# Layer 0's first modulation chunks by pairs of feature tiles, and a 512-column projection between them

## The chip, the core and the metric

The kernel runs on one core of a Trainium2 chip. A core has a matrix engine (PE, whose weight loads are listed as PEld), a vector engine (VectorE, DVE), a scalar engine (ScalarE, ACT), a general engine (GpSimd, POOL) and SyncE (SP), which issues the DMA transfers. The metric is device time in microseconds (us), median over runs.

## The reference

Two transformer layers over 512 latent tokens and 256 context tokens, 1024 features. In each layer an input projection feeds an attention part and a gated MLP part; then come an output projection, and a squared-ReLU MLP. Both normalisations are modulated: shift, scale and gate are computed from a conditioning vector by one large matrix `w_mod`.

```python
m_lat = silu(c) @ w_mod[l] + b_mod[l]          # 6 x 1024: sh1, sc1, ga1, sh2, sc2, ga2
m_ctx = silu(c_ctx) @ w_mod[l] + b_mod[l]
h_lat = rmsnorm(x_lat, norm1_g[l]) * (1 + sc1) + sh1
h_ctx = rmsnorm(x_ctx, norm1_g[l]) * (1 + csc1) + csh1
z = h @ w_in[l]                                 # 512 q | 128 k | 128 v | 512 u | 512 g
q, k = rope(rmsnorm(q)), rope(rmsnorm(k))       # rope on latents alone
attn = softmax(q k^T) v                         # latents see all keys, context sees context
gm = gelu(u) * (w_s @ layernorm(gelu(g)) + b_s) # mixing inside chunks of 128 tokens
x = x + ga1 * (concat(attn, gm) @ w_out[l])
x = x + ga2 * (relu(modulate(rmsnorm(x))) ** 2 @ ...)   # w_ff1, w_ff2
```

## The kernel before

The residual `X` lies feature by token: eight tiles of 128 features x 768 tokens (512 latents, 256 context), two in each of four buffers. Every product is made at near float32 precision from three matmuls: each operand is split into a high and a low part (`hi`, `lo`), and hi x hi, hi x lo and lo x hi are summed in PSUM. A weight block of 128 x 1024 is loaded as `raw`; `split` casts it to `hi` on ScalarE and subtracts on VectorE to get `lo`. `block_order` writes down in which order blocks are loaded; `pump` issues the loads on SP while fewer than `RING` = 4 blocks are live, `take` hands them out, `release` gives them back. The first blocks go into buffers that are free at the start (`EARLY`, buffers A, B, C). In the start phase splits are held back (`held`) and made by `convert`.

PSUM has three pools of two buffers: `pa` (two banks each), `pb` and `pt` (one bank each).

`mod_chunk(l, j)` multiplies 512 columns of layer 0's `w_mod`, eight matmuls in float32 (two PE instructions each), with the conditioning vectors as the 32 columns of the weights. So several run side by side in PE's column groups: two for the first four chunks (`NS` = 2), four for the others. VectorE transposes the sums, eight tiny matmuls with a selection matrix (`fin`) bring the result into feature order, and `mod_store` adds the bias and makes `Amod` = (1 + scale) * gain. Chunks 0 and 1 are the shift of features 0 to 511 and 512 to 1023, chunks 2 and 3 the scale.

`Norm` makes one normalisation: squares on ScalarE (`step`), added up over the eight feature tiles on VectorE or POOL (`acc`); `sums` adds over partitions by one-column matmuls against `ones` and takes the reciprocal root; `bcast` spreads it over partitions; `apply` makes the modulated `h` tile by tile (VectorE, then a cast on ScalarE to the high part, then VectorE for the low part).

`start`, whose PE and VectorE order is that of the program text, runs: squares and `acc` of the latents, chunk 0, `sums`, chunk 2, first weight block, `apply` of tiles 0 to 3, chunk 1, then chunk 3 in quarters with the projection of keys and values (256 columns, `TokProj.wide`) for tiles 0 to 3 between them, then `apply` and projection of tiles 4 and on. After it the scheduler orders the engines by priority (the order of the text) and readiness.

`layer` then runs PLAN[0]: latent parts of u tiles 0 and 1 (`w0`, `w1`), context part of tile 0 (`x0`), keys and values of context (`kv`), the g projections A0 to B2 by pairs of token tiles with u tiles between, and after them the queries in two groups of 256 columns, three `bank` calls each. A bank is one PSUM buffer: `pt` if `self.early`, else `pb`; `self.early` is true if `kv0` is None when the projection is made, which holds before for the first one alone. Each bank goes to a sink: `qk` (normalisation of heads and rotation), `sink_g` (gelu, layer norm, later `mixing` into a `pt` buffer). Keys and queries are stacked (`stack`) and transposed (`turn`, two `pt` buffers) some 10 us later by the kernel's own clock `fl`.

Of the kernel before, what the change touches and what calls it, by code (L numbers as in the profile page):

```python
# [117 lines left out]
EARLY = [f"A{i}" for i in range(7, 3, -1)] + [f"B{i}" for i in range(7)] + ["C0", "C1"] + [f"A{i}" for i in range(7, 3, -1)]  # L118
PLAN = (("w0", "w1", "x0", "kv", "A0", "u2", "A1", "A2", "x1", "B0", "B1", "B2"),
# [3 lines left out]
def block_order():  # L123
    o = []
    mod = lambda j: [("mod", 0, j, kb) for kb in range(0, 4, 1 if j < 4 else 2)]
    tok = lambda l, g: [("tok", l, g, kb) for kb in range(2)]
    for l in range(DEPTH):
        if l == 0:
            o += mod(0) + mod(2) + tok(0, 0)[:1] + mod(1) + mod(3) + [("ctx",)] * (not PAR["XO"]) + tok(0, 0)[1:] + [("ctx",)] * PAR["XO"]
# [7 lines left out]
        o += tok(l, 1) + tok(l, 2)  # L137
# [24 lines left out]
    return o  # L162
# [3 lines left out]
def trunk(ctx: ExitStack, tc: tile.TileContext, xT, pk1, pk2, rope, wsT, w_mod, w_tok, w_u, w_out, w_ff1, w_ff2, outT):  # L166
# [53 lines left out]
    RING = 4  # L220
# [110 lines left out]

    def mod_chunk(l, j, lag=1200.0):
# [3 lines left out]
        ns = PAR["NS"] if j < 4 else 4  # L336
        rows = ns * 32
        for kb in range(0, 4, ns // 2):
            ws_ = take("mod", l, j, kb)[:ns // 2]
# [18 lines left out]
        if lag:  # L358
            fl.defer(lag, fin)
        else:  # L360
            fin()
# [48 lines left out]
    def mod_store(l, j, src, nc_=2):  # L410
        b0 = PK1["bmod"][0] + l * 48 + j * 4
# [21 lines left out]
    class Norm:  # L433
# [5 lines left out]
        def step(self, k):  # L439
# [6 lines left out]
            sq = (tw if self is cx and PAR['SQ'] else tsm)([128, n])  # L446
# [4 lines left out]
        def sums(self, *others):  # L451
# [55 lines left out]
    class TokProj:  # L507
        def __init__(self, l, grp, h, npair, sink):
            self.h, self.npair, self.sink, self.left = h, npair, sink, npair
            self.key = ("tok", l, grp)  # L510
            self.wb = {}
            self.early = PAR["BK"] == 1 and kv0 is None

        def passes(self, k):
            if k // 4 not in self.wb:
                self.wb[k // 4] = take(*self.key, k // 4)
# [36 lines left out]

    DENSE = {0: ((0, 384), (384, 384)), 1: ((0, 512),)}
# [17 lines left out]
    def consts(l):  # L572
        k2 = const.tile([128, 640], F32, tag="k2", name=nm("k2"))
        nc.scalar.dma_start(k2, pk2[l])
# [17 lines left out]
        vec.tensor_scalar_mul(P2("bs"), P2("bs"), 0.5)  # L592
# [5 lines left out]
    def layer(l, h, nxt, K, kv=None, kv0=0):  # L598
# [11 lines left out]
        def qk(ps4, tp, nh, which):  # L610

            sq = tsm([128, 2, nh, 64])
            act.activation(sq, ps4, AF.Square)
# [3 lines left out]
            if tp < 2:  # L617
# [6 lines left out]
                (pool_e if l in PAR['R1'] else vec).tensor_tensor(out=t1, in0=t1, in1=t2, op=ALU.add)  # L624
# [4 lines left out]
            r = rsqrt(ss, 2 * nh, l)  # L629
            (pool_e if l in PAR['R2'] else vec).tensor_tensor(out=t1, in0=t1, in1=r.rearrange("p (a b) -> p a b", b=nh).unsqueeze(3).broadcast_to([128, 2, nh, 64]), op=ALU.mult)  # L630
# [76 lines left out]
        def u_part(m, part):  # L707
# [4 lines left out]
            ps = (pt if PAR["BK"] == 2 and m and not part else pb)()[:, 0:n]  # L712
# [376 lines left out]
    def start():  # L1089
        nonlocal held  # L1090
        for k in range(KT):
            lat.step(k)
        run(mod_chunk(0, 0, PAR["S0"]))
        lat.sums()
        run(mod_chunk(0, 2, PAR["S2"]))
        convert()
        lat.bcast()
        fl.tick(PAR["S2"])
        lat.apply(h0, range(4))
        kv0.passes(0)  # L1100
        run(mod_chunk(0, 1, PAR["S1"]))
        for k in range(KT if PAR['CL'] == 0 else 0):
            cx.step(k)
        g = mod_chunk(0, 3, 1.0)
        for k in range(4):
            next(g)
            if k == 3:
                convert()
            kv0.wide([k])
            fl.tick()  # L1110
        fl.tick(1.0)
        lat.apply(h0, range(4, KT), lambda k: convert() if k == 6 else None)
        for k in range(KT if PAR['CL'] == 1 else 0):
            cx.step(k)
        if PAR["CS"] == 0:
            cx.sums()
        kv0.wide(range(4, PAR["KB"]))
        if PAR["CS"] == 1:
            cx.sums()

    if PAR["KF"]:
        pump()
# [3 lines left out]
    kv0 = TokProj(0, 0, h0, 3, None)  # L1126
    ET = mybir.EngineType
    MSS = {1: {ET.PE}, 2: {ET.PE, ET.Activation}, 3: {ET.PE, ET.DVE}, 4: {ET.PE, ET.DVE, ET.Activation}}
    if PAR["MS"]:
        with tc.manual_schedule(engines=MSS[PAR["MS"]]):  # L1130
            start()
    else:
        start()
# [6 lines left out]
    layer(0, h0, h1, K0, kv0, PAR["KB"])  # L1140
# [6 lines left out]
def _layout(x, c, ctx, c_ctx, w_mod, b_mod, norm1_g, w_in, q_norm_g, k_norm_g, gmlp_norm_g, w_spatial, b_spatial,  # L1147
# [20 lines left out]
    o["w_mod"] = C(A(w_mod).reshape(L, 4, 2, 128, 12, 512).transpose(0, 4, 1, 3, 2, 5).reshape(L, 12, 4, 128, 1024))  # L1168
# [4 lines left out]
    o["w_tok"] = C(wt.reshape(L, 2, 4, 128, 5, 256).transpose(0, 4, 1, 3, 2, 5).reshape(L, 5, 2, 128, 1024))  # L1173
# [25 lines left out]
```

## Time and profile before

| | |
|---|---|
| median of 3 runs | 1500.83 us (1500.49 to 1501.65) |
| profiled execution, first to last instruction | 1500.4 us |
| its instructions | 22327 |
| PE busy | 1460.4 us (97%) |
| VectorE busy | 893.1 us (60%) |
| ScalarE busy | 640.1 us (43%) |
| POOL busy | 340.4 us (23%) |
| moved by DMA | 148.80 MB, mean 99 GB/s |

The profiled execution is one run of the program; its own time is the span, and the runs' times are 0.1 to 1.3 us longer. A timeline row is: start, length, engine, line, operation, output <- inputs, shape, number of instructions merged; in brackets the idle time of the engine before it and what ended that. A row of the waits is: who waited for whom, total us, times, longest. `PEclk` is the clock granted to PE as a share of full speed. Tile names leave out buffer numbers: `A<-in_w_mod` is a load of modulation weights into a buffer A.

### The profile page before, as it was taken

How to read it: one execution, taken by the hardware profiler on the slowest of the kernel's cores; microseconds unless marked ns; L12 is line 12 of the kernel's file. 1: busy time of each engine (PE TensorE's matmuls, PEld its weight loads, DVE VectorE, ACT ScalarE, POOL GpSimd, SP SyncE). 2: the span in 40 equal slices, each digit the busy share in tenths (PEclk: the TensorE clock that was granted, in tenths of full speed). 3: DMA queues.
4: the chain of work that ended last, by engine and by line, in shares of the span. 5: the costliest groups of instructions: out<-in, count | busy, mean ns of one | idle time of the engine just before them, and what ended most of it. 6: DMA issues, size and time to landing. Idle time of an engine off the chain costs nothing.

```text
span 1500.4 us, 22327 instructions
## 1 busy us (share of the span) xinstructions
PE 1460.4 (97%) x8770; PEld 1286.8 (86%) x8770; DVE 893.1 (60%) x1667; ACT 640.1 (43%) x1078; POOL 340.4 (23%) x324
## 2 busy tenths in 40 slices
PE   6899999999999999999999999999999999999998
PEld 2899887798889999898989988997889888888887
DVE  5878767787755554544444436866877544444443
ACT  3443455674545443424334224536774333322221
POOL 0112331222064452313232213156222000000000
PEclk9999999999999999999999999999999999999999
DMA  9221454201233333433333311321001323333331
GB/s 365 65 77 38 175 182 146 90 15 57 74 118 116 112 115 116 131 109 123 117 115 124 99 43 57 99 71 57 29 1 57 114 97 98 99 99 99 99 96 73
DMA packets 49945, 148.80 MB, mean 99 GB/s; under 512 B 5424, under 2 KB 6832, under 8 KB 49840
## 3 DMA queue, kind: packets, MB, share of 16 engines
q1 hardware_dynamic: 49264, 146.46, 29.5%
q8 instruction: 69, 1.13, 0.3%
q10 hardware_dynamic: 576, 0.92, 0.2%
q14 instruction: 36, 0.29, 0.1%
HBM read 145.26 MB, written 2.10 MB: 98 GB/s over the span
## 4 chain that ended last, share of the span: by engine, by line
PE 88%; DVE 4%; DMA 2%; POOL 2%; ACT 2%; issue 1%; SPq 0%; POOLq 0%; ACTq 0%; DVEq 0%
PE pa L208 52%; PE pb L208 27%; PE pt L877 3%; PE pt L208 2%; PE pb L343 1%; PE pt L648 1%; DMA raw<-in_w_tok 1%; DMA B<-in_w_mod 1%; POOL acc L449 1%; DMA A<-in_w_mod 1%; DVE A L483 1%; DVE s L487 1%; DVE X L817 1%; POOL m L289 0%; DVE B L997 0%
## 5 line engine op out<-in xcount | busy, mean ns | idle before, releaser
L208 PE MATMUL pa<-A,hi 128*128 128x384 f32 (+2 forms) x1696 | 449.2, 347 | 2.1 <-DVE s L702 0.8
L212 ACT CAST hi<-raw 128x1024 fp32r<-128x1024 f32 x171 | 179.5, 1050 | 464.5 <-PE pa L208 378.7
L213 DVE TENSOR_TENSOR lo<-raw,hi 128x1024 fp32r<-128x1024 f32 x155 | 195.8, 1263 | 230.9 <-ACT hi L212 227.5
L208 PEld LDWEIGHTS pa<-A,hi 128*128 128x128 f32 x1696 | 304.4, 188 | 26.4 <-ACT w L990 2.0
L208 PE MATMUL pa<-A,lo 128*128 128x384 f32 (+2 forms) x848 | 293.5, 346 | 1.1 <-DVE lo L213 1.1
L208 PE MATMUL pa<-B,hi 128*128 128x512 f32 (+1 forms) x900 | 239.7, 355 | 2.7 <-DVE X L817 2.7
L387 POOL TENSOR_TENSOR C<-C,s 128x512 f32<-128x512 f32 x112 | 162.9, 1469 | 316.3 <-ACT s L386 275.6
L208 PEld LDWEIGHTS pa<-B,hi 128*128 128x128 f32 x900 | 158.7, 188 | 30.7 <-DVE X L817 4.9
L208 PEld LDWEIGHTS pa<-A,lo 128*128 128x128 f32 x848 | 159.4, 188 | 12.1 <-DVE lo L213 1.5
L817 DVE SCALAR_TENSOR_TENSOR X<-pa,modT,X 128x512 f32<-128x512 f32 x126 | 82.9, 660 | 141.8 <-PE pa L208 141.8
L208 PE MATMUL pb<-B,hi 128*128 128x512 f32 (+1 forms) x600 | 157.8, 351 | 3.8 <-DVE X L817 3.8
L208 PE MATMUL pa<-B,lo 128*128 128x512 f32 (+1 forms) x450 | 157.7, 354 | 0.0
L208 PE MATMUL pb<-hi,A 128*128 128x256 f32 x672 | 126.4, 285 | 0.8 <-DVE s L702 0.8
L817 DVE SCALAR_TENSOR_TENSOR X<-pb,modT,X 128x512 f32<-128x512 f32 (+3 forms) x116 | 71.0, 619 | 85.4 <-PE pb L208 85.0
L208 PEld LDWEIGHTS pb<-B,hi 128*128 128x128 f32 x600 | 105.0, 191 | 18.4 <-DVE X L817 5.3
L208 PEld LDWEIGHTS pb<-hi,A 128*128 128x128 f32 x672 | 106.2, 191 | 1.0 <-PE pb L208 1.0
L208 PE MATMUL pb<-B,lo 128*128 128x512 f32 (+1 forms) x300 | 104.9, 350 | 0.0
L386 ACT ACTIVATE s<-k,silu 128x512 f32<-128x512 f32 x112 | 76.8, 716 | 45.3 <-DMA k<-in_w_mod 36.2
L208 PE MATMUL pb<-lo,A 128*128 128x256 f32 x336 | 95.1, 283 | 0.0
L208 PEld LDWEIGHTS pa<-B,lo 128*128 128x128 f32 x450 | 84.0, 188 | 11.3
L208 PE MATMUL pb<-A,hi 128*128 128x512 f32 (+2 forms) x288 | 81.5, 363 | 2.1 <-POOL A L808 2.1
L880 DVE TENSOR_TENSOR A<-pt,A 128x384 fp32r<-128x384 f32 (+1 forms) x144 | 73.0, 536 | 10.5 <-ACT A L879 8.9
(176 smaller groups left out, 2209.5 us busy)
## 6 DMA issues: line engine op xcount, KB each, us to landing
raw<-in_w_ff SPq DMA_DIRECT2D x128, 512.0 KB, 3.5
k<-in_w_mod SPq DMA_DIRECT2D x96, 256.0 KB, 3.1
raw<-in_w_tok SPq DMA_DIRECT2D x19, 512.0 KB, 3.4
raw<-in_w_out SPq DMA_DIRECT2D x16, 512.0 KB, 3.5
lo<-in_w_mod SPq DMA_DIRECT2D x16, 512.0 KB, 4.6
hi<-in_w_mod SPq DMA_DIRECT2D x16, 512.0 KB, 3.9
A<-in_w_mod SPq DMA_DIRECT2D x8, 512.0 KB, 9.7
raw<-in_w_u SPq DMA_DIRECT2D x8, 512.0 KB, 3.4
```

Of the source, the lines that this page charges most:

```text
L208: pe.matmul(out, a, b, start=start, stop=stop)
L212: act.copy(hi, src)
L213: (eng or vec).tensor_tensor(out=lo, in0=src, in1=hi.bitcast(F32), op=ALU.subtract)
L343: pe.matmul(ps[q:q + 32, :], S32[:, k, :], ws_[k2 // 2][:, k2 % 2 * 512:(k2 % 2 + 1) * 512], start=k < ns, stop=k >= KT - ns)
L386: act.activation(p, w, AF.Copy, scale=s)
L387: pool_e.tensor_tensor(out=a, in0=a, in1=p, op=ALU.add)
L449: eng.tensor_tensor(out=self.acc, in0=self.acc, in1=sq, op=ALU.add)
L483: (pool_e if k % 2 < PAR['LP'].get('%d%d%d' % (l, w, off // 256), 0) else vec).scalar_tensor_tensor(out=h[k][:, 1, off:off + n], in0=t, sc ...
L487: vec.scalar_tensor_tensor(out=t, in0=xk(k)[:, off:off + n], scalar=Amod[l][w][:, k, cond:cond + 1], in1=self.bc[:, 0:n], op0=ALU.mult, op ...
L817: vec.scalar_tensor_tensor(out=xs, in0=src[:, s - off:e - off], scalar=modT[l][:, i * 8 + m, cond:cond + 1], in1=xs, op0=ALU.mult, op1=ALU ...
L877: pe.transpose(tp_[:, (kt - k0) * 128:(kt - k0) * 128 + 128], p[:, kt * 128:kt * 128 + 128], ident)
L880: vec.tensor_tensor(out=ptl[:, k0:k0 + step, d], in0=src, in1=pth[:, k0:k0 + step, d].bitcast(F32), op=ALU.subtract)
```

## The change

Layer 0's columns of `w_mod` for the first normalisation are laid out anew: chunk c holds shift and scale of features 256c to 256c + 255, two feature tiles, and `mod_store` writes both. All chunks run four matmuls side by side. The first 512 columns of the token projection (keys, values, half of the queries) are laid out by feature tiles, two per block, and `WideProj` multiplies them as 512-column matmuls, latents in the start phase and context later. `start` now runs, for each chunk: pieces of `h` for its two tiles, projection of the first, second half of the next chunk, projection of the second with the chunk's `fin` in the middle, first half of the chunk after that. The sums of squares of the latents are made by one-column matmuls on each squared tile, accumulated in PSUM. The ring has five slots. The sinks of keys, values and the first queries use POOL for add, root and multiply. `kv0` is no longer assigned.

```diff
-PLAN = (("w0", "w1", "x0", "kv", "A0", "u2", "A1", "A2", "x1", "B0", "B1", "B2"),
+AB = ["A7", "A6", "A5", "A4"], ["B1", "B2", "B3", "B4"]
+EARLY = AB[0] + ["B0"] + AB[1] + ["B5"] + AB[0] + ["B6"] + AB[1] + ["C0"]
+PLAN = (("w0", "kv", "x0", "u1", "A0", "u2", "A1", "A2", "B0", "B1", "B2"),
...
-            o += mod(0) + mod(2) + tok(0, 0)[:1] + mod(1) + mod(3) + ...
+            for c in range(4):
+                o += mod(c) + [("tok", 0, c)]
+            o += [("ctx",)]
...
-    RING = 4
+    RING = 5
...
+                nc.sync.dma_start(k2s[0][:, 128:640], pk2[0][:, 128:640])
...
-        ns = PAR["NS"] if j < 4 else 4
+        ns = 4
...
+        def pieces(self, h, k):
+            ...
+            t = tsm([128, n])
+            vec.scalar_tensor_tensor(out=t, in0=xk(k)[:, off:off + n], scalar=Amod..., in1=self.bc[:, 0:n], op0=ALU.mult, op1=ALU.mult)
+            act.activation(h[k][:, 0, off:off + n], t, AF.Identity, bias=B)
+            return lambda: vec.scalar_tensor_tensor(out=h[k][:, 1, off:off + n], in0=t, scalar=B, in1=h[k][:, 0, off:off + n].bitcast(F32), op0=ALU.add, op1=ALU.subtract)
...
+    class WideProj:
+        def __init__(self, h):
+            self.h, self.wb = h, {}
+            self.ps = [pa().rearrange("p (t n) -> p t n", t=2) for _ in range(2)]
...
+        def latents(self, k, mid=None):
+            for t in range(4):
+                if t == 2 and mid:
+                    mid()
+                for i, (a, b) in enumerate(self.passes(k, slice(t * 128, t * 128 + 128))):
+                    mm(self.ps[t // 2][:, t % 2, :], a, b, k == 0 and i == 0, k == KT - 1 and i == 2, 512)
+            fl.tick()
+
+        def context(self):
+            ps = [pb(), pb()]
...
-            r = rsqrt(ss, 2 * nh, l)
-            (pool_e if l in PAR['R2'] else vec).tensor_tensor(out=t1, ...
+            r = rsqrt(ss, 2 * nh, l or pool)
+            (pool_e if pool or l in PAR['R2'] else vec).tensor_tensor(out=t1, ...
...
+        def both(tp, ps):
+            sink_kv(tp, ... 0:256 ..., True)
+            q0(tp, ... 256:512 ..., True)
...
-            ps = (pt if PAR["BK"] == 2 and m and not part else pb)()[:, 0:n]
+            ps = pt()[:, 0:n]
...
+                elif s == "kv" and l == 0:
+                    for tp in range(2):
+                        both(tp, kv.ps[tp])
+                    both(2, kv.context())
...
-            for g in range(2):
-                qp = TokProj(l, 1 + g, h, NP, sink_q(g))
+            for g in range(2) if l else (1,):
+                qp = TokProj(l, 1 + g, h, NP, sink_q(g) if g else q0)
...
     def start():
+        ps = [pa() for _ in range(2)]
+        chunk = [mod_chunk(0, c, None) for c in range(4)]
         for k in range(KT):
-            lat.step(k)
...
+            sq = tsm([128, SEQ])
+            act.activation(sq, xk(k)[:, 0:SEQ], AF.Square)
+            if k == KT - 1:
+                next(chunk[0])
+            for t in range(4):
+                pe.matmul(ps[t // 2][:, t % 2 * 512:t % 2 * 512 + 1], sq[:, t * 128:(t + 1) * 128], ones[:, 0:1], start=k == 0, stop=k == KT - 1)
+        v = small(4)
+        for i in range(2):
+            vec.tensor_scalar(v[:, 2 * i:2 * i + 2], ps[i]..., 1.0 / D, EPS, op0=ALU.mult, op1=ALU.add)
+        r = rsqrt(v, 4, 1)
+        next(chunk[0])
+        lat.diag(r)
+        fins.pop()()
         lat.bcast()
+        next(chunk[1])
+        kvq = WideProj(h0)
+        for c in range(4):
+            k = 2 * c
+            lows = []
+            if c:
+                convert()
+            lows.append(lat.pieces(h0, k))
+            if not c:
+                convert()
+                lows.pop()()
+            lows.append(lat.pieces(h0, k + 1))
+            for f in lows:
+                f()
+            if c == 3:
+                convert()
+                kvq.latents(k)
+                kvq.latents(k + 1, cx.sums)
+                break
+            if c == 2:
+                for i in range(KT):
+                    cx.step(i)
+            kvq.latents(k)
+            next(chunk[c + 1])
+            kvq.latents(k + 1, lambda: fins.pop()())
+            if c < 2:
+                next(chunk[c + 2])
...
-    kv0 = TokProj(0, 0, h0, 3, None)
...
-    nc = _bacc.Bacc("TRN2", target_bir_lowering=False, num_devices=1)
+    nc = _bacc.Bacc("TRN2", target_bir_lowering=False, num_devices=1, dynamic_dma_scratch_size=2048)
```

More of the change, by code (lines that the diff above doesn't have):

```diff
@@ L125, in block_order @@
     mod = lambda j: [("mod", 0, j, kb) for kb in range(0, 4, 1 if j < 4 else 2)]
-    tok = lambda l, g: [("tok", l, g, kb) for kb in range(2)]
+    tok = lambda l, g: [("tok", l, 2 * g + kb) for kb in range(2)]
     for l in range(DEPTH):
         if l == 0:
-            o += mod(0) + mod(2) + tok(0, 0)[:1] + mod(1) + mod(3) + [("ctx",)] * (not PAR["XO"]) + tok(0, 0)[1:] + [("ctx",)] * PAR["XO"]
+            for c in range(4):
+                o += mod(c) + [("tok", 0, c)]
+            o += [("ctx",)]
         else:
@@ L357, in fin @@
             mod_store(l, j, p4)
-        if lag:
+        if lag is None:
+            fins.append(fin)
+        elif lag:
             fl.defer(lag, fin)
@@ L410, in mod_store @@
     def mod_store(l, j, src, nc_=2):
+        if l == 0 and j < 4:
+            two = slice(2 * j, 2 * j + 2)
+            bm = c1[:, PK1["bmod"][0]:PK1["bmod"][0] + 16].rearrange("p (s k) -> p s k", s=2)
+            vec.tensor_tensor(out=modT[0][:, 0:16, :].rearrange("p (s k) c -> p s k c", s=2)[:, :, two, :], in0=src.rearrange("p (s k) c -> p s k c", s=2),
+                              in1=bm[:, :, two].unsqueeze(3).broadcast_to([128, 2, 2, 2]), op=ALU.add)
+            g0 = PK1["ng"][0] + 2 * j
+            vec.scalar_tensor_tensor(out=Amod[0][0][:, two, :], in0=modT[0][:, 8 + 2 * j:10 + 2 * j, :], scalar=1.0,
+                                     in1=c1[:, g0:g0 + 2].unsqueeze(2).broadcast_to([128, 2, 2]), op0=ALU.add, op1=ALU.mult)
+            return
         b0 = PK1["bmod"][0] + l * 48 + j * 4
@@ L515, in passes @@
             if k // 4 not in self.wb:
-                self.wb[k // 4] = take(*self.key, k // 4)
+                self.wb[k // 4] = take("tok", self.l, 2 * self.grp + k // 4)
             hi, lo = self.wb[k // 4]
@@ L551, in wide, with passes @@
                     self.sink(tp, self.ps[tp][:, :, 0:256])
+    class WideProj:
+        def __init__(self, h):
+            self.h, self.wb = h, {}
+            self.ps = [pa().rearrange("p (t n) -> p t n", t=2) for _ in range(2)]
+        def passes(self, k, ts):
+            if k // 2 not in self.wb:
+                self.wb[k // 2] = take("tok", 0, k // 2)
+            hi, lo = (w[:, k % 2 * 512:k % 2 * 512 + 512] for w in self.wb[k // 2])
+            hk = self.h[k]
+            return (hk[:, 0, ts], hi), (hk[:, 0, ts], lo), (hk[:, 1, ts], hi)
+        def latents(self, k, mid=None):
[7 more added lines that the diff above has]
+            ps = [pb(), pb()]
+            for k in range(KT):
+                for t in range(2):
+                    for i, (a, b) in enumerate(self.passes(k, slice(SEQ + t * 128, SEQ + t * 128 + 128))):
+                        mm(ps[t], a, b, k == 0 and i == 0, k == KT - 1 and i == 2, 512)
+                if k % 2:
+                    release()
+                fl.tick()
+            return ps
     DENSE = {0: ((0, 384), (384, 384)), 1: ((0, 512),)}
@@ L608, in layer, with qk @@
         Q = []
-        def qk(ps4, tp, nh, which):
+        def qk(ps4, tp, nh, which, pool=False):
             sq = tsm([128, 2, nh, 64])
-            act.activation(sq, ps4, AF.Square)
+            if isinstance(ps4, list):
+                for t in range(2):
+                    act.activation(sq[:, t], ps4[t], AF.Square)
+            else:
+                act.activation(sq, ps4, AF.Square)
             ss = small(2 * nh)
@@ L623, in qk @@
                     vec.tensor_tensor(out=t2[:, :, :, o], in0=ps4[:, :, :, i], in1=bcast(G[:, which, 1, tp * 2:tp * 2 + 2, o]), op=ALU.mult)
-                (pool_e if l in PAR['R1'] else vec).tensor_tensor(out=t1, in0=t1, in1=t2, op=ALU.add)
+                (pool_e if pool or l in PAR['R1'] else vec).tensor_tensor(out=t1, in0=t1, in1=t2, op=ALU.add)
+            elif isinstance(ps4, list):
+                g = P2(("qg", "kg")[which]).unsqueeze(1).broadcast_to([128, nh, 64])
+                for t in range(2):
+                    vec.tensor_tensor(out=t1[:, t], in0=ps4[t], in1=g, op=ALU.mult)
             else:
@@ L1104, in start @@
[L1104 to L1107, printed above, removed]
-                convert()
[L1109 to L1119, printed above, removed]
@@ L1123, in trunk @@
+        P2 = K0[0]
+        vec.tensor_scalar_mul(P2("bs"), P2("bs"), 0.5)
+        return kvq
+    k2s = [const.tile([128, 640], F32, tag="k2", name=nm("k2"))]
+    pump()
     K0 = consts(0)
@@ L1125, in trunk @@
     h0 = [unit(f"A{k}", [128, 2, T]) for k in range(8)]
-    kv0 = TokProj(0, 0, h0, 3, None)
[L1127 to L1133, printed above, removed]
+    with tc.manual_schedule(engines={ET.PE, ET.DVE}):
+        kvq = start()
     while held:
@@ L1139, in trunk @@
     h1, K1 = [], []
-    layer(0, h0, h1, K0, kv0, PAR["KB"])
+    layer(0, h0, h1, K0, kvq)
     layer(1, h1, None, K1[0])
```

85 lines of the change are left out of this document (50 added, 35 removed).

## The prediction

> **What bounds the kernel now.** I read the page first, then busy time by stretch, then the timeline of the first 100 us and PE's waits. The page:
>
> ```profile
> span 1500.4 us, 22327 instructions
> PE 1460.4 (97%) x8770; PEld 1286.8 (86%) x8770; DVE 893.1 (60%) x1667; ACT 640.1 (43%) x1078; POOL 340.4 (23%) x324
> ```
>
> PE is busy for 97% of the span, so only PE work saved, or PE time lost, can move the end. By stretch (its length, busy time of PE, PEld, DVE, ACT and POOL, granted clock, DMA share, GB/s):
>
> ```profile
> 12.00:30.00 18.00, 16.08 (x80) 4.45 (x80) 11.16 (x27) 3.92 (x6) 0.00 (x0) 1.00 1.03 409
> ...
> 60.00:80.00 20.00, 19.82 (x147) 18.63 (x147) 18.93 (x66) 13.23 (x27) 1.69 (x2) 1.00 0.19 56
> ```
>
> Up to 30 us the DMA engines are full (409 GB/s, share 1.03) and PE has nothing but modulation matmuls and sums. From 60 us on PE is full (19.82 of 20). So the change is worth what it does to the first 60 us, and what it may spoil later. The start, from the timeline:
>
> ```profile
> 7.26 0.63 ACT L444 ACTIVATE acc<-X 128x512 f32<-128x512 f32 x1 [3.20 <-DMA X<-in_xT]
> ...
> 15.23 0.21 PEld L343 LDWEIGHTS pb<-A,S 128*32 128x32 f32 x2 [0.64 <-DMA A<-in_w_mod]
> 16.09 0.21 PEld L343 LDWEIGHTS pb<-A,S 128*32 128x32 f32 x2 [0.64 <-issue]
> 16.80 0.13 PEld L343 LDWEIGHTS pb<-A,S 128*32 128x32 f32 x2 [0.51 <-DMA A<-in_w_mod]
> 17.23 0.13 PEld L343 LDWEIGHTS pb<-A,S 128*32 128x32 f32 x2 [0.30 <-issue]
> 18.20 0.97 PEld L458 LDWEIGHTS pt<-ones,acc 128*128 128x128 f32 x8 [0.84 <-issue]
> ...
> 44.10 1.01 PE L458 MATMUL pt<-ones,acc 128*128 128x1 f32 x4 [3.91 <-POOL acc L449]
> 44.98 0.56 PE L208 MATMUL pa<-hi,A 128*128 128x256 f32 x1
> ```
>
> The reader sees two clocks. Modulation pairs follow each other in 0.86 us (15.23 to 16.09), after 16.8 in 0.43 (16.80 to 17.23): PE starts at half speed, though the stretch's clock column says 1.00. The sum over features with a one-column matmul (L458) costs 0.97/8 = 0.12 us an instruction at full speed and (44.98 - 44.10)/4 = 0.22 at half speed. The idle 3.9 us before 44.1 had brought the half clock back.
>
> **The change, part by part.**
>
> *1. Sums of squares on PE.* VectorE's adds go (L449); each squared tile goes through four one-column matmuls, eight instructions. All stand in PE's order ahead of chunk 0's two halves (the first half before tile 7's). What does PE's clock do meanwhile? Two places where it had been lowered:
>
> ```profile
> 44.00:47.40 3.40, 3.30 (x15) 3.30 (x16) 3.21 (x5) 3.15 (x5) 0.05 (x1) 0.50 0.00 0
> 47.40:50.85 3.45, 3.45 (x17) 3.35 (x16) 3.30 (x6) 1.33 (x2) 0.00 (x0) 0.51 0.29 76
> 921.20:924.60 3.40, 3.40 (x18) 3.40 (x18) 2.99 (x4) 0.84 (x2) 2.94 (x2) 0.50 0.32 108
> 924.60:928.00 3.40, 3.25 (x27) 3.07 (x27) 1.03 (x3) 1.35 (x2) 1.17 (x2) 1.00 0.61 200
> ```
>
> At 921 one stretch full of wide matmuls brings the full clock back. At 44 the stretch is as busy, but its first 0.88 us are L458, and it takes a second one. I read it so: one-column matmuls don't count as work for the clock. Then PE stays at half speed through all sums. From 7.95 (end of the first square): seven tiles x 8 x 0.214 (0.22, at the exact half of the matmul pace) = 12.0, to 20.0; half of chunk 0, two rounds of 0.86, to 21.7; tile 7, 1.7, to 23.4; second half to 25.1. Before, chunk 0 was through at 18. This hides nothing; it is the new path. The weights of chunk 0 land by 17 (its last pair starts at 17.23), those of chunk 1 five transfers of 0.52 MB later, 6.4 us at 409 GB/s: neither sets it any more.
>
> The Trainium skill, page "TensorE: Matmul & The Clock Gate", section "Part 1: The HAM clock gate", states otherwise: the warm-up is some 3.4 us of time, whatever is issued in it. By that rule the sums themselves raise the clock at about 13; the sum for it stands below as a rival.
>
> *2. Four chunks in four column groups* (NS=4 for all): a half is then two rounds instead of four, so each chunk costs 1.7 us at full clock, not 3.4. Not on the path before (DMA was), half on it now.
>
> *3. The chain from a chunk to its projection*, by these rows of PE, VectorE and ScalarE, each from its engine's timeline:
>
> ```profile
> 23.04 0.66 PE L476 MATMUL pt<-c,w 128*128 128x128 f32 x4
> 23.92 0.24 PE L356 MATMUL pt<-w,c 64*32 64x8 f32 x8 [0.22 <-DVE w L351]
> 23.16 0.71 DVE L351 STREAM_TRANSPOSE w<-pb 64x512 f32<-64x512 f32 x1 [1.39 <-PE pb L343]
> 23.90 1.22 DVE L213 TENSOR_TENSOR lo<-B,hi 128x1024 fp32r<-128x1024 f32 x1
> ...
> 27.65 0.74 DVE L487 SCALAR_TENSOR_TENSOR s<-X,A,pt 128x512 f32<-128x512 f32 x1
> 28.30 0.75 DVE L483 SCALAR_TENSOR_TENSOR A<-s,modT,A 128x512 fp32r<-128x512 f32 x1
> 28.42 0.72 ACT L488 ACTIVATE A<-s,modT 128x512 fp32r<-128x512 f32 x1 [0.82 <-DVE s L487]
> ```
>
> Chunk 0: 25.3 transpose 0.7, diagonal 0.4, broadcast at half clock about 1.2 (0.66 doubled), to 27.7; scaled tile 0.74 and cast 0.72, to 29.2; weight split and low part on VectorE, 1.2 + 0.7, to 30.4. The reciprocal root on POOL has the second half and the transpose as cover, 2.5 us; what it took beyond that would lie on the path. Chunk 1's first half fits in between. Twelve 512-column matmuls then need 2.7 us at full clock; with the clock back at about 32.5 (one full stretch after 27.4 to 30.8) tile 0 ends at 33.4 and the half chunk at 34.3. From there each pair repeats: selection, store 0.4, split 1.2 (1.15 to the next start), scaled tile 0.7, cast 0.75, low part: 3.8 us, in which PE has half a tile (1.4) and half a chunk (0.9). PE work of one pair is 5.5 + 1.7 + 0.2 = 7.4, idle 1.1, together 8.5. Tile 1 ends at 37.3, tile 3 at 45.9, tile 5 at 54.4, tile 7 (longer wait, since no half chunk is left to fill it) at 62.6. The idle gaps stay below 2 us, so I don't expect the clock to fall again.
>
> *4. What PE has done by then.* Rates (start, length, count in the chain; two rows for 384 columns):
>
> ```profile
> 56.76 7.99 PE pb L208 x35
> 64.75 5.03 PE pt L208 x42
> ```
>
> ```profile
> 81.28 0.51 PE L208 MATMUL pa<-A,hi 128*128 128x384 f32 x2
> 85.44 0.28 PE L208 MATMUL pb<-hi,A 128*128 128x256 f32 x1
> ```
>
> 512 columns 0.228 us, 256 columns 0.120, 384 columns (85.44 - 81.28)/24 = 0.173. Before: at 64.6 the latent keys and values and both latent u tiles are done; context keys and values (48 x 0.120), the two context u parts (48 x 0.120) and half the queries (144 x 0.120) remain: 28.8, to 93.4. After: u0 to 68.1, then 48 x 0.228 context keys, values and queries, 24 x 0.120, and u1 48 x 0.173: 22.2, to 90.3. Of this the 512-column form gives 144 x (0.240 - 0.228) = 1.7; the rest is order. Gain 3.1; less 0.3 for the context's broadcast, which was before 64.6, less 0.4 for a clock that comes back late: **2.4**.
>
> *5. Moved work.* The sinks come much earlier for half the queries, and for these and the keys add, root and multiply go to POOL. VectorE loses the nine small operations of each root and has u0, context and u1 as cover (5.5 + 10.9 + 8.3 us of PE). Without that cover its load (18.93 of 20 us at 60 to 80) would show. PE's waits on these sinks and on split weights:
>
> ```profile
> PE pa L208 <- DVE lo L213: 1.1, 1, 1.1
> PE pa L208 <- DVE s L702: 0.8, 1, 0.8
> PE pb L208 <- DVE s L702: 0.8, 1, 0.8
> ```
>
> The two of 0.8 stand between the projections and attention, and half the queries are now done long before: 0 to 1.6, I take 0.8.
>
> *6. Fifth ring slot, `k2`'s split DMA, smaller DMA scratch.* The wait of 1.1 above is all that PE loses on weights, so the slot brings at most that: I take 0. The second load of A7 to A4 now waits on SP for chunk 0 (25.1), and what is queued behind it, tok 2 and chunk 3, waits too; one transfer lands like this, from the page's DMA issues (median us):
>
> ```profile
> A<-in_w_mod SPq DMA_DIRECT2D x8, 512.0 KB, 9.7
> ```
>
> Chunk 2's second half, issued at 25.1, is there by 35 and needed at 42, so this is hidden; on a path 7 us faster it would begin to show.
>
> *7. Banks.* `kv0` now stays None, so `TokProj.early` is true for every projection and all `bank` calls take `pt`, not `pb`, in both layers. They share two buffers with turns and mixings (rows of ScalarE, VectorE, PE, VectorE):
>
> ```profile
> 81.48 0.60 ACT L697 ACTIVATE s<-pb 128x512 f32<-128x512 f32 x1 [0.32 <-PE pb L208]
> 83.50 0.69 DVE L702 SCALAR_TENSOR_TENSOR s<-s,pb 128x512 f32<-128x512 f32 x1 [0.70 <-ACT s L699]
> 96.60 1.45 PE L208 MATMUL pt<-ws,B 128*128 128x128 f32 x12
> 98.09 0.88 DVE L769 SCALAR_TENSOR_TENSOR s<-pt,gnh,k 128x256 f32<-128x256 f32 x2 [1.57 <-PE pt L208]
> ```
>
> A bank is held 2.7 us past its matmuls (81.48 to 84.19); the next runs 48 x 0.120 = 5.8, so 3.1 us are left in which one mixing (96.6 to 98.97, 2.4 us) just fits. Eighteen banks in the two layers. Lower bound 0, since u tiles in `pa` can fill PE and ring slot five brings them nearer; upper bound below. I take 1.3, near the lower end.
>
> Sum: 2.4 + 0.8 - 1.3 = 1.9. The profiled execution's span of 1500.4 lies 0.4 under the median of 1500.8, which is kept: **1498.9**.
>
> **Rivals.** *(a) The sums do raise the clock.* A stretch of 3.4 us begins between 7.95 and 11.4, so the clock is back at 13 on average: three tiles by then, four more in 32 x 0.12, half, tile 7, half: chunk 0 done at 19.8 instead of 25.1, and the halves, broadcast and tile 0 after it at full clock, another 1.9: 7.2 us, 1491.7. For it: PE's records there are gapless. Against it: the stretch at 44.
>
> *(b) The `pt` banks decide, slower.* If a mixing and a turn of like length come between two banks, 4.8 us want into 3.1 and PE stands for up to 1.7; I take 1.2. Without any such stall the sum is 1497.6. At three places of 18 the gain is gone, from six on (7.2 us, 1504.8) the kernel is slower by more than 0.2%, and with nine it takes 1508. For it: VectorE, whose reads free the buffers, is busy for 18.93 of 20 us at 60 to 80. Against: all other PE work is free to move up.
>
> *(c) No order matters: the DMA limit holds.* Latents, four chunks and four blocks are 24 transfers of 0.52 MB, 12.6 MB, 31 us at 409 GB/s and some 35 with the slower first microseconds; the chain above reaches the last at 46 to 54. So the DMA no longer ends last, and this would give no more than the forecast.
>
> **How the numbers follow.** A change under 0.2%, 3 us, can't be told from none here. Forecast 1498.9, chance 0.65, own range 1495.5 to 1502.5 (the chain's 8.5 us a pair may be off by 0.7 a time, clock return 30.4 to 37): a third of it faster (0.21), 0.40 same, 0.04 slower. (a) 0.20, nearly all faster. (b) 0.15, of it 0.12 slower. (c) changes nothing. Faster 0.40, same 0.44, slower 0.16. Range 1490.5 to 1504.5.
>
> **What would show it.** Right: one-column matmuls from 8 us at 0.21 us an instruction, chunk 0's second half ending near 25, first 512-column matmul near 29, last latent one near 62, PE full from there. Wrong: full clock before 16 us (a); waits of PE on `pt` readers between 90 and 150 or near 1000 to 1100 (b); first 512-column matmul waiting on a w_mod or w_tok DMA (c); the clock at one half between 35 and 62, which would cost 1.7 us for each 3.4.

## The result, and the profile after

The changed kernel takes **1537.07 us** (median of 5 runs, 1533.53 to 1539.1) against 1500.49 (5 runs): ratio 1.0236, 95% interval 1.022 to 1.0251. It is 2.4% slower, and far outside the forecast range. The page of the changed kernel:

```profile
span 1535.3 us, 22099 instructions
PE 1478.6 (96%) x8682; PEld 1297.0 (84%) x8682; DVE 882.3 (57%) x1593; ACT 638.7 (42%) x1081; POOL 360.8 (23%) x341
```

By totals hardly anything shows: PE is still busy for 96%, with 18 us more of busy time from fewer instructions. Some 13 of these 18 are the sums of squares at the start (12.07 us below and 1.8 for tile 7, against 1.05 before); matmuls at half clock, which count as busy, are part of the rest. The start first, PE's timeline:

```profile
7.68 12.07 PE L1192 MATMUL pa<-ones,s 128*128 128x1 f32 x56 [7.68 <-ACT s L1188]
19.69 1.93 PE L348 MATMUL pb<-A,S 128*32 128x512 f32 x8
...
23.35 1.93 PE L348 MATMUL pb<-A,S 128*32 128x512 f32 x8
...
29.36 0.54 PE L211 MATMUL pa<-hi,A 128*128 128x512 f32 x1
...
57.49 0.50 PE L211 MATMUL pa<-hi,A 128*128 128x512 f32 x1 [1.93 <-ACT A L495]
...
63.65 0.40 PE L211 MATMUL pa<-hi,A 128*128 128x512 f32 x1
```

The sums take 12.07/56 = 0.216 us each, chunk 0's second half ends at 25.3, the first 512-column matmul starts at 29.4, the last latent one ends at 64. That is the forecast chain, within 1.5 us. The loss comes later. By stretch, the kernel before and then the changed one (length, busy time of PE, PEld, VectorE, ScalarE, POOL, granted clock, DMA share, GB/s):

```profile
80.00:100.00 20.00, 19.88 (x147) 19.68 (x146) 10.17 (x33) 7.50 (x14) 2.97 (x3) 1.00 0.16 51
100.00:120.00 20.00, 19.17 (x163) 19.00 (x161) 17.98 (x67) 7.54 (x12) 4.79 (x4) 1.00 0.25 79
140.00:160.00 20.00, 20.00 (x171) 20.00 (x171) 18.00 (x57) 6.55 (x11) 5.69 (x6) 1.00 0.24 79
160.00:180.00 20.00, 18.63 (x134) 16.70 (x132) 14.55 (x46) 7.12 (x14) 4.27 (x5) 1.00 0.49 175
```

```profile
80.00:100.00 20.00, 14.62 (x88) 13.65 (x87) 12.95 (x28) 7.98 (x17) 14.94 (x12) 0.94 0.33 105
100.00:120.00 20.00, 14.75 (x88) 13.30 (x87) 4.85 (x11) 10.21 (x21) 6.68 (x6) 0.89 0.08 27
140.00:160.00 20.00, 16.37 (x133) 15.91 (x132) 16.01 (x58) 6.62 (x10) 7.29 (x5) 1.00 0.16 54
160.00:180.00 20.00, 17.14 (x116) 16.69 (x116) 13.06 (x52) 3.15 (x6) 4.68 (x5) 0.83 0.29 106
...
1000.00:1100.00 100.00, 94.58 (x627) 86.48 (x627) 61.93 (x128) 49.83 (x91) 47.25 (x40) 0.93 0.20 66
```

PE, full before, stands for a quarter of the time from 80 to 120, and the clock falls below 1.00 in three of the four stretches. POOL is busy for 14.94 of 20 us from 80 to 100, where it had 2.97. What PE waits for between 80 and 300 in the changed kernel (total us, times, longest; before, the four largest were 0.8, 0.8, 0.6 and 0.5):

```profile
PE pt L724 <- POOL k L712: 8.7, 3, 4.9
PE pt L211 <- DVE s L792: 6.0, 4, 2.8
```

The first row is `turn`, waiting for the low part that POOL makes in `stack`; the second a bank in `pt`, waiting until VectorE, making the gelu of an earlier bank, has read that bank for the last time. A third, 3.4 us of attention's transposes (L971) behind ScalarE's exponential, is as long in e2 below and 0.3 in e1 and e3; why it goes with the banks is open. In layer 1, between 1000 and 1110, PE's waits ahead of work in `pt` are five rows of 5.5 us in all (e1: one of 1.0); the first is that of matmuls that wait for the read of a mixing:

```profile
PE pt L211 <- DVE s L859: 2.1, 2, 1.1
```

In the timeline the waits of layer 0 have their places:

```profile
97.34 0.77 PE L724 MATMUL pt<-c,k 128*128 128x128 f32 x4 [4.88 <-POOL k L712]
...
114.94 1.97 PE L724 MATMUL pt<-c,k 128*128 128x128 f32 x8 [2.46 <-POOL k L712]
...
153.37 0.36 PE L211 MATMUL pt<-hi,A 128*128 128x256 f32 x1 [2.81 <-DVE s L792]
```

The first two gaps are each followed by a stretch at half clock (stretches cut at the clock's changes); the third, 2.81 us long, is not, and the clock stays full until 162.6:

```profile
94.60:98.00 3.40, 0.66 (x5) 0.66 (x6) 0.54 (x3) 0.35 (x2) 2.73 (x4) 0.96 0.00 0
98.00:101.40 3.40, 3.40 (x14) 3.30 (x14) 1.45 (x4) 2.28 (x8) 0.83 (x2) 0.53 0.00 0
...
111.70:115.10 3.40, 0.94 (x9) 0.70 (x7) 1.78 (x2) 2.69 (x5) 1.30 (x1) 0.96 0.08 19
115.10:118.50 3.40, 3.40 (x17) 3.18 (x18) 0.51 (x1) 1.59 (x3) 0.00 (x0) 0.54 0.40 140
```

The gap of 2.46 us so costs 2.46 and another 1.7. To place losses I count, in each trace, the PE work still to do (every matmul at its full-clock price: 0.228, 0.173, 0.120 or 0.112 us by columns, modulation 0.112) and compare the moments at which two kernels have the same amount left. Difference to the kernel before, in us, at the moments of the kernel before that head the columns:

| kernel (named as below) | 93.8 | 105.7 | 146.8 | 192.5 | 283.7 | 983 | 1048 | end |
|---|---|---|---|---|---|---|---|---|
| changed | +4.2 | +13.8 | +20.5 | +26.8 | +28.8 | +30.5 | +35.1 | +34.8 |
| e1: banks in `pb` | +6.7 | +10.4 | +10.4 | +25.0 | +26.9 | +25.1 | +23.3 | +23.0 |
| e3: and no POOL | +1.2 | +3.4 | +3.3 | +15.8 | +17.7 | +16.4 | +14.9 | +14.3 |
| e5: and late mixings | -1.3 | +0.9 | +0.9 | +6.3 | +8.3 | +7.0 | +7.3 | +6.7 |
| e6: and sums on VectorE | -5.5 | -3.3 | -3.3 | +2.7 | +4.7 | +2.9 | +1.9 | +1.3 |
| e4: before, banks in `pt` | -0.2 | +1.4 | +10.5 | +13.9 | +13.8 | +22.7 | +28.7 | +28.7 |

The loss sits between 94 and 195 us, in layer 0's sinks and g projections, and for banks in `pt` again near 1000 to 1050, in layer 1's. Each line is one profiled execution (e6's is the quickest of its runs, 1503.57, those of e1 and e4 the longest of theirs), and they differ by chance as well: e3 and e5 have the same start, and yet 2.5 us lie between them at 93.8. So a line is good to some 2 us, and the medians below decide.

### The profile page after: what moved, and what is told of

It reads as the page before. It is cut to its first block, busy times and chain, and to the rows that moved or that the text cites. A ratio compares the mean times of both kernels' runs of the same rounds, so it can differ in the third digit from the quotient of the medians.

```text
span 1535.3 us, 22099 instructions
## 1 busy us (share of the span) xinstructions
PE 1478.6 (96%) x8682; PEld 1297.0 (84%) x8682; DVE 882.3 (57%) x1593; ACT 638.7 (42%) x1081; POOL 360.8 (23%) x341
## 4 chain that ended last, share of the span: by engine, by line
PE 83%; DVE 7%; ACT 4%; POOL 3%; issue 2%; DMA 1%; POOLq 0%; SPq 0%; ACTq 0%; DVEq 0%
PE pa L211 51%; PE pb L211 18%; PE pt L211 8%; PE pt L971 3%; PE pb L348 2%; POOL m L292 1%; PE pa L1192 1%; DVE lo L216 1%; PE pt L724 1%; ACT hi L215 1%; DVE A L513 1%; DVE X L911 1%; DVE s L517 1%; DVE B L1091 1%; ACT w L955 0%
## 5 line engine op out<-in xcount | busy, mean ns | idle before, releaser
L211 PE MATMUL pa<-A,hi 128*128 128x384 f32 (+2 forms) x1728 | 459.2, 348 | 3.4 <-ACT w L1084 1.0
L211 PEld LDWEIGHTS pa<-A,hi 128*128 128x128 f32 x1728 | 310.7, 189 | 27.8 <-ACT w L1084 2.7
L211 PE MATMUL pa<-A,lo 128*128 128x384 f32 (+2 forms) x864 | 299.2, 347 | 0.0
L211 PEld LDWEIGHTS pa<-A,lo 128*128 128x128 f32 x864 | 162.8, 189 | 10.7
L211 PE MATMUL pt<-hi,A 128*128 128x256 f32 x576 | 115.0, 297 | 8.2 <-DVE s L792 5.7
L211 PEld LDWEIGHTS pt<-hi,A 128*128 128x128 f32 x576 | 97.0, 204 | 10.3 <-issue 7.8
L211 PE MATMUL pt<-lo,A 128*128 128x256 f32 x288 | 84.9, 295 | 0.0
L973 ACT CAST A<-pt 128x384 fp32r<-128x384 f32 (+1 forms) x144 | 64.2, 469 | 31.0 <-PE pt L971 27.4
```

What stands on the lines that cost most here:

```text
L211: pe.matmul(out, a, b, start=start, stop=stop)
L973: act.copy(pth[:, k0:k0 + step, d], src)
```

## The experiments

**Banks and POOL (e1 to e4).** Theory B: the `pt` banks of part 7 cost the time. Theory P: the sinks on POOL do. e1 puts the banks back in `pb`, e2 takes POOL out of the first sinks, e3 does both, e4 puts the banks of the kernel before in `pt`.

```diff
 e1, e3   -            self.early = PAR["BK"] == 1 and kv0 is None
          +            self.early = False
 e2, e3   -            sink_kv(tp, ..., True);  q0(tp, ..., True)
          +            sink_kv(tp, ..., False); q0(tp, ..., False)
 e4 (on the kernel before)
          +            self.early = True
```

> The changed kernel with the projections' banks back in pb (early = False). Theory B (the shared pt buffers cost the 36 us): 1505 to 1512, waits of PE on gelu reads of pt (8.9 us) and lowered clock between 90 and 290 gone. Theory P (the sinks and stacks on POOL, with the turns that PE's order puts ahead of other work, cost it): 1525 to 1533, the wait of 8.7 us on the POOL stack stays.

> The changed kernel with add, root and multiply of the moved sinks back on VectorE, banks left in pt. Theory B: 1528 to 1537. Theory P: 1505 to 1515, with the waits of PE's turns on the POOL stack gone.

> Both undone; what is left is the new start, the 512-column projection and the fifth slot. If B and P together are the whole loss: 1497 to 1502, since PE has at 90 us about 0.8 us less work left than before at the same time. If the earlier half of the queries itself costs (turns in the way, VectorE over-full), 1505 or more.

> The kernel before with nothing changed but that all banks take pt. Theory B: 1515 to 1530, slower by most of the 36 us. Theory P: 1500 to 1505.

Measured: e1 1521.89 us (ratio to before 1.0147, 1.0127 to 1.0167), e2 1534.88 (1.0229, 1.0209 to 1.0249), e3 1516.27 (1.0106, 1.0086 to 1.0125), e4 1527.48 (1.0178, 1.0158 to 1.0198). So the banks cost 15.2 us in the changed kernel and 26 in the kernel before: the line `kv0`, which reads as tidying up, is the dearest part. POOL costs 5.6 (e1 to e3), and while the banks are wrong hardly anything (2.2, inside the intervals). e2 and e4 fall into the ranges of B, e1 between those of B and P; neither theory alone is the whole loss. e3 leaves 1.06%, the outcome foreseen there if the earlier queries themselves cost.

Why a `pt` bank waits, e4 shows best. PE's two dearest gaps between 100 and 140, then VectorE around the first (the first row of a run of some 20, nearly all layer normalisation, and the row behind them):

```profile
118.23 0.35 PE L208 MATMUL pt<-hi,A 128*128 128x256 f32 x1 [3.00 <-DVE s L769]
136.47 0.55 PE L208 MATMUL pt<-hi,A 128*128 128x256 f32 x1 [2.38 <-DVE s L702]
```

```profile
112.70 0.47 DVE L743 BATCH_NORM_STATS2 bn<-s 128x6 f32<-128x128 f32 x2
...
117.22 0.87 DVE L769 SCALAR_TENSOR_TENSOR s<-pt,gnh,k 128x256 f32<-128x256 f32 x2
```

The mixing's result lies in a `pt` buffer until L769 has read it, and L769 stands in VectorE's order behind 4.6 us of normalisation (112.70 to 117.3) of the last bank. The mixing ended at 115.2, so the read comes 2 us late. As long as `pt` serves mixings and turns alone, that late read costs nothing; with a bank in the other buffer it stops PE.

In the changed kernel the longest of these waits (2.81, at 153.37) has the same cause, but the late read is that of the bank itself. ScalarE and VectorE:

```profile
147.91 0.60 ACT L787 ACTIVATE s<-pt 128x512 f32<-128x512 f32 x1 [2.65 <-PE pt L211]
150.12 1.11 DVE L839 TENSOR_SCALAR s<-s,mv,m 128x128 f32<-128x128 f32 x4
151.16 0.68 DVE L788 SCALAR_TENSOR_TENSOR s<-s,pt 128x512 f32<-128x512 f32 x1
152.53 0.69 DVE L792 SCALAR_TENSOR_TENSOR s<-s,pt 128x512 f32<-128x512 f32 x1 [0.30 <-ACT s L789]
```

VectorE normalises the bank before until 151.2, and this bank is held for 5.3 us, from 147.91 to 153.22, where the prediction had 2.7. The next two waits of this kind, 1.43 each at 162.30 and 172.72, follow banks held for 2.7 as predicted, with a mixing in the other buffer.

**What e3 still loses (e5).** In e3 PE waits here, from its timeline:

```profile
166.68 0.69 PE L211 MATMUL pt<-ws,B 128*128 128x128 f32 x2 [5.44 <-ACT B L215]
```

```profile
161.10:174.80 13.70, 7.54 (x35) 7.22 (x35) 9.29 (x40) 1.22 (x2) 3.40 (x4) 0.51 0.00 0
```

That is a mixing. The second query group's sink runs all outstanding ones at its first bank, to get their buffers. Before, the first query group (three banks of 48 x 0.120, 17 us) stood between g bank B2 and that place; with it done in the start phase, the second group follows B2 at once, and the mixing needs the gelu, the normalisation and the split that B2's result has only just begun. The clock then stays at half for 13.7 us. In the changed kernel itself PE's waits show no such row; it comes up once the banks are in `pb` (5.5 us in e1, 5.7 in e3). e5 lets the second group run the mixings at its last bank:

```diff
+            def room():
+                if len(Q) < grp * 2 + 2:
+                    ...   (the mixings, then the buffers)
             def f(tp, ps, pool=False):
-                if tp == 0:
-                    ...
+                if tp == (NP - 1 if grp and l == 0 else 0):
+                    room()
```

> The run with banks in pb and no work on POOL, and one more edit: in layer 0 the second group of queries no longer makes the g mixings run at its first pair of token tiles; they run when its last pair comes, or when its first turn is due. Theory M (the 12 us that were still lost between 150 and 182 us of that run are PE waiting for the gelu, layer norm and split of the last g bank, because with half of the queries done earlier nothing stands between that bank and its mixing; the half clock after the gap makes it dearer): 1503 to 1507, and no PE gap over 3 us between 140 and 190. Rival K (the earlier queries and their turns cost in themselves, or the scarcity of other PE work moves the gap somewhere else): 1512 to 1518, with a gap of like length at another place before 200 us.

Measured: 1510.10 us (1.0072, 1.0054 to 1.0089), 6.2 less than e3, between the two expectations. The 5.4 us wait is gone; of the 12 us that e3 lost between 147 and 192, some 5 remain, most of them in a gap between g banks, of 2.96 us at 155.6, and the half clock after it. From PE's waits of e5 from 80 to 300:

```profile
PE pb L211 <- DVE s L801: 3.0, 1, 3.0
```

**The sums of squares (e6, e7).** e6 is e5 with the latents' squares added up on VectorE again:

```diff
-            ... one-column matmuls on each squared tile
+            lat.step(k)
+        next(chunk[0]); lat.sums(); next(chunk[0])
```

> The run before this one, and the latents' sums of squares added up on VectorE again, with four one-column matmuls at the end instead of 56 on the path. Theory (the one-column matmuls hold chunk 0 back until 25 us and keep PE's clock at half): chunk 0's second half ends at 18 to 20, the first 512-column matmul starts at 22 to 24, the last latent one ends some 6 us earlier, and the time is 5 to 7 us under that of the run before it, about 1498. Rival D (a path faster by 6 us meets the DMA: chunk 2's second half, chunk 3 and blocks land too late): the first 512-column matmul is early but later ones wait on w_mod or w_tok transfers, and the gain is 0 to 3 us.

Measured: 1505.36 us (1503.57 to 1509.77; ratio 1.0047, 1.0032 to 1.0063), 4.7 less than e5 and just short of the 5 to 7 expected. Its start, from PE's timeline:

```profile
14.55 1.05 PE L479 MATMUL pt<-ones,acc 128*128 128x1 f32 x8
15.53 1.06 PE L348 MATMUL pb<-A,S 128*32 128x512 f32 x8
...
21.86 0.80 PE L211 MATMUL pa<-hi,A 128*128 128x512 f32 x1
...
58.64 0.40 PE L211 MATMUL pa<-hi,A 128*128 128x512 f32 x1
```

The first 512-column matmul comes 7.5 us earlier than in the changed kernel, the last one 5; the DMA does not stop it.

e7 puts 16 wide matmuls ahead of the sums of the changed kernel, to see what the clock counts:

```diff
+        wm, wp = tsm([128, SEQ]), pt()
+        vec.memset(wm, 1.0)
+        for _ in range(8):
+            pe.matmul(wp[0:32], wm[:, 0:32], wm, start=True, stop=True)
+            pe.matmul(wp[32:64], wm[:, 0:32], wm, start=True, stop=True)
```

> The changed kernel with 16 additional 512-column matmuls on PE ahead of the one-column sums; their result is not used. One question: what raises and holds PE's clock. My reading (one-column matmuls do not count as work for the clock): the clock is full for at most one or two stretches of 3.4 us after the wide ones, then half again during the sums; chunk 0's second half ends near 20 or later. Rival, the rule of the Trainium skill, page 'TensorE: Matmul & The Clock Gate', section 'Part 1: The HAM clock gate' (whatever is issued counts, and only idle time lowers the clock): the clock stays full through the sums, an instruction of them takes 0.12 us throughout, and the second half ends near 17.5. Either way the total goes down by 3 to 8 us against the changed kernel, to 1529 to 1534.

```profile
11.43 9.49 PE L1197 MATMUL pa<-ones,s 128*128 128x1 f32 x56
...
24.51 1.93 PE L348 MATMUL pb<-A,S 128*32 128x512 f32 x8
```

```profile
11.43:14.80 3.37, 3.37 (x30) 3.37 (x29) 0.00 (x0) 2.33 (x4) 0.00 (x0) 0.93 1.03 411
14.80:18.20 3.40, 3.40 (x17) 3.40 (x18) 0.00 (x0) 1.42 (x4) 0.00 (x0) 0.50 1.02 406
```

PE is never idle from 11.43 to 20.8, yet the clock, raised by the wide matmuls, falls back to one half after one stretch of one-column ones, and chunk 0's halves take 1.93 us as at half clock. So one-column matmuls neither raise the clock (the changed kernel's 56 at 0.216 us) nor hold it. The expected gain in time did not come (1538.8, one run): the wide matmuls held the first sum back from 7.68 to 11.43, and chunk 0 ended at 26.4 instead of 25.3.

**The fifth slot (e8).**

```diff
 (on the kernel before)
-    RING = 4
+    RING = 5        # and the smaller DMA scratch
```

> The kernel before with five ring slots instead of four and the smaller DMA scratch, nothing else. My step (the slot is worth nothing, since PE loses 1.1 us on weights in the whole run): 1499 to 1503. Rival (a fifth block loaded and split earlier takes ScalarE and VectorE away from sinks, and is part of what the change loses): 1506 or more.

Measured: 1500.89 us (1.001, 1.0001 to 1.002). Priced rightly at next to nothing, as far as the kernel before shows it.

**Where e6's lead goes (e10, e11, e13).** e6 leads by 5.5 us at 94 and has lost it by 192. Three orders of the plan, to put work without a sink where PE waits:

```diff
 e6   "w0", "kv", "x0", "u1", "A0", "u2", "A1", "A2", "B0", "B1", "B2"
 e10  "w0", "kv", "x0", "u1", "A0", "A1", "A2", "u2", "B0", "B1", "B2"
 e11  "w0", "kv", "x0", "u2", "A0", "w1", "A1", "A2", "B0", "x1", "B1", "B2"
 e13  "w0", "kv", "x0", "u1", "A0", "A1", "A2", "B0", "B1", "u2", "B2"
```

> The best run so far (banks in pb, no work on POOL, late mixings, sums on VectorE), with u tile 2 moved in the plan of layer 0 from behind A0 to behind A2. Theory (PE still loses some 3 us before 95 and 5 us between 151 and 158, where the last g bank waits for a pb buffer, because too little work that needs no sink is left there; u tile 2 is 8.3 us of such work): the wait of 3.0 on the pb reader at L801 and the half clock behind it go, 4 to 5 us less: 1500 to 1502. Rival (the g banks cannot go faster than VectorE and ScalarE let them, 9.4 us a bank, and u tile 2 is missing at A1 and A2 instead): 1504 to 1508, with a new pb wait of 2 to 3 us before 135.

> The same base, with u tile 2 ahead of A0 and u tile 1 split as in the kernel before: its latent part behind A0 and its context part behind B0. Theory: u tile 2 (8.3 us) covers the turns of keys and first queries at 85 to 95 better than u tile 1 in pt, whose buffers the turns need, and the two parts of u tile 1 fill the places between g banks; 1498 to 1501. Rival (as above, a cover that is moved is missing at the place it leaves): 1504 or more.

> The same base, with u tile 2 behind B1. Theory: it stands directly ahead of the bank that waits, B2, so that the wait of 3.0 goes; but the scheduler may take it earlier for any other wait of a bank; 1500 to 1503. Rival (the rate of the g banks decides): 1504 or more, with the wait at another bank.

Measured: e10 1506.47 us (1.0038, 1.0024 to 1.0053), e11 1505.72 (1.0037, 1.0022 to 1.0051), e13 1520.19 (1.0117, 1.0099 to 1.0135). By the time the rival holds each time, though the new waits are not where it put them. In e10 the `pb` wait of 3.0 has gone and these stand in its place, for the `pa` buffer of a u tile (1.4 in e6) and for a mixing (PE's waits from 60 to 220):

```profile
PE pa L211 <- DVE s L801: 2.5, 1, 2.5
PE pt L211 <- ACT B L215: 2.1, 1, 2.1
```

In e13 the profiled execution (1520.36) has one wait of 7.7 at 143.6, for the `pa` buffer of u tile 2. The work that needs no sink is the same in all four, and I read it so: moved, it is missing where it was. No run puts the first queries back into their old place, so that their move costs e6 the rest is argued, not shown.

**A gap filled (e12).** What half clock costs by itself, on the kernel before:

```diff
+        wp = pt()
+        for i in range(14):
+            pe.matmul(wp, h0[i % 4][:, 0, 0:128], h0[i % 4][:, 0, 0:512], start=True, stop=True)
         if PAR["CS"] == 0:
             cx.sums()
```

> The kernel before with 14 additional 512-column matmuls on PE in the gap of 3.9 us at 40 (behind chunk 3, ahead of the context's sums of squares); their result is not used. Theory (an idle gap costs twice: its own length, and the half clock that follows it, here 6.8 us long, 3.4 us lost): the gap is filled at no cost, the granted clock stays full from 44 to 51, the four one-column matmuls take 0.5 us instead of 1.0, and the time is 3 to 4 us lower, 1496 to 1498. Rival (the stretch at half speed is given back, because PE then waits for the modulated tiles, whose engines set the pace there): 1499.5 to 1501.

```profile
39.77 3.47 PE L1117 MATMUL pt<-A 128*128 128x512 f32 x14 [0.29 <-DVE modT L412]
```

```profile
44.00:50.85 6.85, 6.50 (x52) 6.44 (x53) 6.48 (x10) 3.83 (x6) 0.00 (x0) 1.00 0.17 48
```

The clock does what was expected, 1.00 in place of 0.50, but the time doesn't follow: 1500.14 us (0.9998, 0.9989 to 1.0007), within the rival's range. Its profiled execution is 2 us ahead of that of the kernel before at 106; but e8's, with no such matmuls and half clock from 44.2 to 47.6 alone, is 1.8 ahead there. VectorE's 6.48 of 6.85 us in that stretch suggest that the tiles of `h` set the pace there, which no run separates.

No version tried beats the kernel before.

## Why the prediction was wrong

Right were parts 1 to 4, the start: sums at 0.216 us (0.214 foretold), chunk 0's end at 25.3 (25.1), the last latent matmul at 64.0 (62.6), and the changed kernel less POOL, banks and mixings (e5) leads by 1.3 us at 94, of 2.4. Some of that is luck. In part 3 a pair took 9.1 to 9.2 us, not 8.5, which is the 1.4 us by which the last tile is late; the clock was back at 29.5, not 32.5, and tile 1 ended at 37.2, where it was foretold, all the same. (The 1.1 us of idle a pair is also mis-added: 3.8 less 1.4 and 0.9 is 1.5. The trace has 0.44 and 0.51, and 1.93 where no half chunk is left.) "The idle gaps stay below 2 us, so I don't expect the clock to fall again" came true in the changed kernel and in e5, but in e1 and e3, with the same start and the same gap, the clock did fall (last section), and e3 is 1.2 us behind at 94.

The Trainium skill, page "TensorE: Matmul & The Clock Gate", section "Part 1: The HAM clock gate", has any issued work warm the clock; e7's rows decide against it, and rival (a) with it. Part 6 was right too (e8). Rival (c) played no part.

1. *Part 7 was mis-sized: 1.3 us stood for 15.2* (26 in the kernel before). I had seen that every bank moves to `pt`, and rival (b) had the mechanism, both layers and the rows that would show it. Three of its sizes failed. The 1.3 is about one stall of 1.2; in the changed kernel PE stands for `pt` for 6.0 us in four waits of layer 0 and 5.5 in six of layer 1. Most are near 1.2 or below it, but a buffer was said to be held for 2.7 us by a bank and 2.4 by a mixing: where VectorE comes to the read late, behind a normalisation, PE stands for 2.81, and for 3.0 in e4. And a stall was priced at its own length; some bring 1.7 us of half clock or more. "All other PE work is free to move up" did not prevent it.

2. *Part 5 had the sign wrong: a gain of 0.8 stood for a loss of 5.6.* The loss is POOL's, with the banks in `pb`; with them in `pt` it is 2.2 (e2), and `turn` still waits 5.8 us there, not 8.7. I counted what VectorE is spared and PE's cover, 24.7 us, but not how long POOL takes for the same chain. Its rows, and VectorE's row for the add in e6:

```profile
90.01 2.35 POOL L696 TENSOR_TENSOR w<-w,s 128x512 f32<-128x512 f32 x1
92.33 1.64 POOL L292 TENSOR_TENSOR m<-m,mhalf 128x8 f32<-128x8 f32 x1
...
96.03 1.26 POOL L712 TENSOR_TENSOR k<-w,k 128x512 fp32r<-128x512 f32 x1
```

```profile
84.95 0.69 DVE L696 TENSOR_TENSOR w<-w,s 128x512 f32<-128x512 f32 x1
```

   The add takes 2.35 us there, 0.69 on VectorE, and stands in order ahead of `stack`'s low part, which `turn` needs; PE waited 4.88.

3. *A wait that I had not named:* the earlier queries take away the work between bank B2 and its mixing, 6.2 us (e3 to e5) once the banks are in `pb`. I priced the sinks that come earlier, not the place they leave. The prediction said "Moved work" and followed it to its new place alone.

4. *The sums on PE cost 4.7 us* (e5 to e6). The forecast had their delay right, as part of the new path, but set no price on it against sums on VectorE; e6's lead at 94 is 5.5 us, e5's 1.3.

By medians: 1537.1 less 15.2, 5.6, 6.2 and 4.7 is 1505.4, e6. The shares hold for this order of undoing; the mixing's wait, for one, is not in the changed kernel. e6's lead of 5.5 us is then spent in waits and half clock between the g banks; that it is for want of matmuls that wait for no sink fits e10 to e13, but is argued. The Trainium skill, same page, section "A second HAM failure mode: psum-queue depth-cycling", tells of another kernel in which short idles between groups of matmuls that cycle through PSUM banks make the clock swing, and the swings cost throughput. This trace agrees between 1000 and 1100, where the changed kernel has a clock of 0.93 and e1, with the banks in `pb`, 1.00:

```profile
1000.00:1100.00 100.00, 98.00 (x694) 89.17 (x693) 71.90 (x147) 56.76 (x108) 50.49 (x46) 1.00 0.18 59
```

## What to carry to other kernels

Where an engine is full, work that can run at any time is its reserve: moving some of it earlier takes cover away from every wait that it stood in front of, so look at the place that is left as closely as at the new one. Before two users share a PSUM pool, find who reads each buffer last and what stands ahead of that read in its engine's order, not how long the read takes. Price a stall of TensorE at its length and, where the clock falls, the half clock after it.

## What the runs showed of the hardware

- Matmuls of one column don't count as work for the clock: it fell to 0.50 with PE 100% busy on them (e7, 14.8 to 18.2 us).
- Gaps shorter than such a stretch of 3.4 us lower the clock too, but not always. The start has one of 1.9 us: in e1, e3 and e6 the clock is at half for 3.4 us soon after it, in the changed kernel and e5 it is not. In each trace the changes of the clock lie whole numbers of 3.41 us apart (3.4, 6.85 and 13.7 us in the rows of this document); counted from them, the gap falls inside one such stretch where the clock drops (e3: 55.5 to 57.4 in 55.1 to 58.5) and is cut in two where it doesn't (changed kernel: 55.6 to 57.5, cut at 56.8). e3, then the changed kernel:

```profile
55.10:58.50 3.40, 1.43 (x5) 0.57 (x4) 3.27 (x5) 1.83 (x3) 1.46 (x1) 1.00 0.00 0
58.50:61.90 3.40, 3.40 (x9) 2.61 (x9) 2.16 (x3) 1.00 (x2) 0.00 (x0) 0.50 0.15 42
```

```profile
53.40:56.80 3.40, 2.16 (x16) 1.21 (x14) 2.72 (x5) 0.08 (x1) 3.05 (x3) 1.00 0.00 0
56.80:60.20 3.40, 2.66 (x10) 1.91 (x11) 3.09 (x4) 2.76 (x4) 0.00 (x0) 1.00 0.01 2
```

- Busy time alone does not decide. In the changed kernel the stretch from 148.95, with PE busy for 1.60 of 3.41 us, kept the full clock, and the one from 159.19, with 1.98, lost it; 1.45 of that were a mixing's matmuls of 128 columns. This fits the first point, that columns count and not time, but no run separates it.

- Sparse work keeps it low: in e3 PE was busy for 7.54 of 13.7 us at half clock before the full one came back.
